# Splitting the first two loads of a streaming SiLU-multiply kernel between two DMA rings: by partition halves in place of rows

## The chip, the cores and the metric

The kernel runs on one core of a Trainium2 chip. The metric is the device time of one execution in microseconds (us); lower is better. The kernel before takes 471.45 us, the median of 3 runs that lie between 471.27 and 471.53 us. Another execution was profiled: it took 471.39 us, and its span, from the first to the last instruction in the trace, is 469.3 us.

## The reference

The input `x` has 32 x 512 rows of 2048 float32 values. Each row is cut in two halves of 1024; the output is SiLU of the first half times the second half.

```python
def reference(x):
    half_dim = x.shape[-1] // 2
    x1, x2 = x[..., :half_dim], x[..., half_dim:]
    silu_x1 = x1 * (1 / (1 + np.exp(-x1)))
    return (silu_x1 * x2).astype(np.float32)
```

The input is 134.22 MB and the output 67.11 MB. Each byte is moved once.

## The kernel before

The 16384 rows are cut into 16 tiles of 1024 rows. A tile puts K = 8 neighbouring rows into each of the 128 partitions, so a partition of an input tile `xt` holds 64 KB that also lie in one piece in memory, and a partition of an output tile `ot` holds 32 KB. There are two buffers for `xt` and two for `ot`. A full input tile is 8 MB (8,388,608 bytes), an output tile 4 MB.

Each tile is loaded, passed through SiLU on ScalarE (`silu`, line 78, from `xt` to `ot`), multiplied in place on VectorE (`mul`, line 85), and stored. The order of the instructions is written out by hand (`manual_schedule`). Two engines start transfers: SyncE (SP in the profile) and ScalarE (ACT). Each has a ring of its own, and the rings feed the same 16 DMA engines; SP's ring is q1 in the trace, ACT's is q10. The rule of the steady part is: SP starts the loads, ACT the stores. After tile i's last multiply, ACT starts the store of tile i and SP the load of tile i+2 into the buffer that has come free (lines 102 to 104).

The beginning is different, because there is no store yet with which loads could share the engines. There both rings carry loads (`load`, lines 67 to 75). Of tile 0, SP takes the first four rows of every partition (4 MB) and ACT the other four. Of tile 1, SP takes six rows of eight (6 MB) and ACT two. SP's part of tile 1 is cut once more into two transfers, one for the even and one for the odd partitions (`LOADED_IN`, line 31). That makes five transfers before the first computation: three on SP, two on ACT. Tile 0 is computed in four chunks of two rows (`KC_FIRST`, line 28), each with a SiLU and a multiply of 128x2048 values.

The end is different too: the last tile is computed in chunks of 2, 2 and 4 rows (`LAST`, line 29), and each chunk is stored by SP as soon as it is multiplied. Behind those stores `settle_all_but` (lines 57 to 65) puts an empty instruction on SP that waits until every transfer has landed except the last n; n is 3 here, the number of the last tile's stores. What then remains open is awaited by the end of the program (line 138).

Of the kernel before, what the change touches and what calls it, by code (L numbers as in the profile page):

```python
# [1 line left out]

# [4 lines left out]


@with_exitstack
def kernel(  # L10
    ctx: ExitStack,
    tc: tile.TileContext,
    x: bass.AP,
    out: bass.AP,
):


    nc = tc.nc
    P = nc.NUM_PARTITIONS

    x_flat = x.flatten_outer_dims()
    out_flat = out.flatten_outer_dims()
    num_rows, in_cols = x_flat.shape
    half = in_cols // 2
    dt = x_flat.dtype

    K = 8
    KC_FIRST = 2
    LAST = (2, 2, 4)
    SHARED = {0: K // 2, 1: 3 * K // 4}  # L30
    LOADED_IN = {1: [slice(0, None, 2), slice(1, None, 2)]}
    PLAN = [K] * (num_rows // (P * K))

    in_pool = ctx.enter_context(tc.tile_pool(name="in_pool", bufs=2))
    out_pool = ctx.enter_context(tc.tile_pool(name="out_pool", bufs=2))

    plan = []
    row = 0
    for k in PLAN:
        plan.append((row, k))  # L40
        row += P * k
    assert row == num_rows
    n_tiles = len(plan)

    def view(flat, i):
        row0, k = plan[i]
        return flat[row0:row0 + P * k].rearrange("(p k) d -> p k d", k=k)

    ctx.enter_context(tc.manual_schedule())

    loaded = {}
    sent = []

    def move(queue, out, in_):
        sent.append(queue.dma_start(out=out, in_=in_).ins)  # L55

    def settle_all_but(n):
        rest = nc.sync.nop(nofuse=True)
        for ins in sent[:-n]:
            tc.add_manual_dep(  # L60
                rest.ins,
                ins.name,
                mybir.DependencyInfo(mybir.DependencyClass.Sync, mybir.DependencyReason.DATA),
                reason="sync sees each earlier transfer land before the last ones",
            )

    def load(i):
        xt = in_pool.tile([P, K, in_cols], dt, name="xt")
        xv = view(x_flat, i)
        cut = SHARED.get(i, K)  # L70
        for ps in LOADED_IN.get(i, [slice(None)]):
            move(nc.sync, xt[ps, :cut], xv[ps, :cut])
        if cut < K:
            move(nc.scalar, xt[:, cut:], xv[:, cut:])
        loaded[i] = xt

    def silu(ot, xt, c, ce):
        nc.scalar.activation(  # L78
            out=ot[:, c:ce, :],
            in_=xt[:, c:ce, :half],  # L80
            func=mybir.ActivationFunctionType.Silu,
        )

    def mul(ot, xt, c, ce):
        nc.vector.tensor_mul(  # L85
            out=ot[:, c:ce, :],
            in0=ot[:, c:ce, :],
            in1=xt[:, c:ce, half:],
        )

    load(0)
    load(1)
    for i in range(n_tiles):
        xt = loaded.pop(i)
        ov = view(out_flat, i)
        ot = out_pool.tile([P, K, half], dt, name="ot")
        if i < n_tiles - 1:
            kc = KC_FIRST if i == 0 else K
            for c in range(0, K, kc):
                silu(ot, xt, c, c + kc)  # L100
                mul(ot, xt, c, c + kc)
            move(nc.scalar, ov, ot)
            if i + 2 < n_tiles:
                load(i + 2)
            continue
        c = 0
        for kc in LAST:
            silu(ot, xt, c, c + kc)
            mul(ot, xt, c, c + kc)
            move(nc.sync, ov[:, c:c + kc], ot[:, c:c + kc])  # L110
            c += kc
        settle_all_but(len(LAST))


# [1 line left out]
_INS = ['x']  # L116
_OUTS = [((32, 512, 1024), 'float32')]


# [23 lines left out]
```

## Time and profile before

| What | Value |
|---|---|
| median of 3 runs | 471.45 us (471.27 to 471.53) |
| the profiled execution | 471.39 us |
| its span | 469.3 us, so 2.1 us lie outside |
| VectorE busy | 139.5 us (30%), 21 multiplies |
| ScalarE busy | 114.2 us (24%), 21 activations and a table load |
| moved by DMA | 201.33 MB, mean 429 GB/s over the span |
| share of ring q1 (SP) and q10 (ACT) in the engines' time | 65.3% and 34.2% |

The profile's page cuts the span into 40 equal slices and gives for each the busy share of every engine and of the DMA engines. The list of waits tells which instruction stood idle and what ended the idle time. The chain that ended last follows the work back from the last instruction, at each step to what released it. The DMA list gives for every kind of transfer its size and the median time from the start of its issue to its landing; a transfer that is queued behind others on its ring counts that time as well. All times within the profile are counted from the start of the span.

### The profile page before, as it was taken

The numbers are of one execution on the slowest core, as the hardware profiler recorded it, in microseconds if no ns is written. First come the engines' busy times: TensorE is split into PE (matmuls) and PEld (weight loads), VectorE is DVE, ScalarE is ACT, GpSimd is POOL, SyncE is SP. The second block draws the span as 40 slices with busy tenths as digits, with TensorE's granted clock in tenths as the row PEclk, the third lists the DMA queues.
The fourth block names the chain that finished last, engine by engine and source line by source line (L and its number), as shares of the span: only waits on it lengthen the run. The fifth ranks groups of instructions, "written<-read, shape, count | busy, mean of one in ns | idle before, by whom it ended". The sixth has DMA issues, their size and how long they took to land.

```text
span 469.3 us, 190 instructions
## 1 busy us (share of the span) xinstructions
DVE 139.5 (30%) x21; ACT 114.2 (24%) x22; POOL 0.2 (0%) x4
## 2 busy tenths in 40 slices
DVE  0070702407024070330704307042070520605142
ACT  1053205032050410504105050050501405014060
POOL 0000000000000000000000000000000000000000
DMA  8999999999999999999999999999999999999988
GB/s 357 424 469 391 458 402 433 416 492 402 413 436 486 408 402 447 486 408 402 444 455 441 402 438 422 480 402 424 424 486 408 405 444 480 413 402 444 466 386 357
DMA packets 5200, 201.33 MB, mean 429 GB/s; under 512 B 592, under 2 KB 592, under 8 KB 592
## 3 DMA queue, kind: packets, MB, share of 16 engines
q1 hardware_dynamic: 2752, 132.12, 65.3%
q10 hardware_dynamic: 2448, 69.21, 34.2%
HBM read 134.22 MB, written 67.11 MB: 429 GB/s over the span
## 4 chain that ended last, share of the span: by engine, by line
DMA 72%; DVE 14%; ACT 12%; ACTq 0%; SPq 0%; issue 0%
DMA xt<-in_x_dram 72%; DVE ot L85 14%; ACT ot L78 12%; ACTq L138 0%; SPq L55 0%; ACTq L78 0%
## 5 line engine op out<-in xcount | busy, mean ns | idle before, releaser
L85 DVE TENSOR_TENSOR ot<-ot,xt 128x8192 f32<-128x8192 f32 (+2 forms) x21 | 139.5, 6659 | 321.4 <-ACT ot L78 321.4
L78 ACT ACTIVATE ot<-xt 128x8192 f32<-128x8192 f32 (+2 forms) x21 | 112.9, 5400 | 340.6 <-DMA xt<-in_x_dram 340.6
L78 ACT ACT_TABLE_LOAD x1 | 1.3, 1283 | 1.6 <-PEq L127 1.6
L127 POOL MEMSET const-bfloat16-1.0<- 128x1 bf16 x1 | 0.1, 101 | 0.0
L127 POOL MEMSET const-uint8-127<- 128x1 uint8 x1 | 0.1, 101 | 0.0
L127 POOL MEMSET const-float32-0.0<- 128x1 f32 x1 | 0.1, 98 | 0.2 <-issue 0.2
L127 POOL MEMSET const-float32-1.0<- 128x1 f32 x1 | 0.1, 98 | 0.0
## 6 DMA issues: line engine op xcount, KB each, us to landing
out_dram<-ot ACTq DMA_DIRECT2D x15, 4096.0 KB, 42.0
xt<-in_x_dram SPq DMA_DIRECT2D x2, 3072.0 KB, 36.4
xt<-in_x_dram ACTq DMA_DIRECT2D x1, 4096.0 KB, 22.1
xt<-in_x_dram SPq DMA_DIRECT2D x1, 4096.0 KB, 21.9
xt<-in_x_dram ACTq DMA_DIRECT2D x1, 2048.0 KB, 41.9
out_dram<-ot SPq DMA_DIRECT2D x2, 1024.0 KB, 7.8
out_dram<-ot SPq DMA_DIRECT2D x1, 2048.0 KB, 7.6
xt<-in_x_dram SPq DMA_DIRECT2D x14, 42.1
```

What stands on the lines that cost most here:

```text
L78: nc.scalar.activation(out=ot[:, c:ce, :], in_=xt[:, c:ce, :half], func=mybir.ActivationFunctionType.Silu,)
L85: nc.vector.tensor_mul(out=ot[:, c:ce, :], in0=ot[:, c:ce, :], in1=xt[:, c:ce, half:],)
L127: nc = _bacc.Bacc("TRN2", target_bir_lowering=False, num_devices=1)
```

## The change

Three things change.

First, the two rings share tiles 0 and 1 in another way. Every transfer now carries whole partitions of 64 KB, all eight rows. SP takes partitions 0 to 63 and ACT partitions 64 to 127, of both tiles; SP's part of tile 1 is cut into partitions 0 to 31 and 32 to 63. The number of transfers at the beginning stays five, three on SP and two on ACT, in the same order.

Second, after these loads are started, VectorE clears one column (`prime`, 128x1) and ScalarE applies SiLU to it, ahead of the first tile's work.

Third, SP's empty instruction at the end awaits all transfers but the last one, so the first two stores of the last tile are among those that it awaits.

```diff
-    SHARED = {0: K // 2, 1: 3 * K // 4}
-    LOADED_IN = {1: [slice(0, None, 2), slice(1, None, 2)]}
+    SHARED = {
+        0: ([slice(0, 64)], [slice(64, P)]),
+        1: ([slice(0, 32), slice(32, 64)], [slice(64, P)]),
+    }
...
         xv = view(x_flat, i)
-        cut = SHARED.get(i, K)
-        for ps in LOADED_IN.get(i, [slice(None)]):
-            move(nc.sync, xt[ps, :cut], xv[ps, :cut])
-        if cut < K:
-            move(nc.scalar, xt[:, cut:], xv[:, cut:])
+        on_sync, on_scalar = SHARED.get(i, ([slice(0, P)], []))
+        for ps in on_sync:
+            move(nc.sync, xt[ps], xv[ps])
+        for ps in on_scalar:
+            move(nc.scalar, xt[ps], xv[ps])
         loaded[i] = xt
...
     load(0)
     load(1)
+    prime = ctx.enter_context(tc.tile_pool(name="prime_pool", bufs=1)).tile([P, 1], dt, name="prime")
+    nc.vector.memset(prime, 0.0)
+    nc.scalar.activation(out=prime, in_=prime, func=mybir.ActivationFunctionType.Silu)
...
-        settle_all_but(len(LAST))
+        settle_all_but(1)
```

## The prediction

> **What bounds the kernel now.** I read the page's slices first, then the chain that ended last, the DMA list, and the stretches between two landings. The slices:
>
> ```profile
> span 469.3 us, 190 instructions
> ...
> DVE 139.5 (30%) x21; ACT 114.2 (24%) x22; POOL 0.2 (0%) x4
> ...
> DMA  8999999999999999999999999999999999999988
> ...
> DMA xt<-in_x_dram 72%; DVE ot L85 14%; ACT ot L78 12%; ACTq L138 0%; SPq L55 0%; ACTq L78 0%
> ```
>
> The DMA engines are busy from end to end, while the two computing engines are idle for 70% and more. The chain shows the same in its links: a tile's work of 15.7 us (SiLU 7.0, multiply 8.7) lets a buffer go, then a load runs for 42 us, and so on. The 42 us are not this transfer alone; the load shares the engines with the load ahead of it and with a store. So one tile costs what its 12.58 MB (8.39 in, 4.19 out) cost on 16 full engines, and the stretches between two landings show it:
>
> ```profile
> 43.20:72.20 29.00, 8.69 (x1) 7.03 (x1) 0.00 (x0) 1.00 1.00 434
> 72.20:101.20 29.00, 8.69 (x1) 7.03 (x1) 0.00 (x0) 1.00 1.00 434
> ...
> 391.20:420.20 29.00, 8.69 (x1) 7.03 (x1) 0.00 (x0) 1.00 1.00 434
> ```
>
> The columns are stretch, length, busy time of VectorE, ScalarE and GpSimd, clock, DMA share, GB/s. Each tile takes 29.00 us at 434 GB/s. All 201.33 MB at this pace are 464.0 us. The first packet starts at 1.74 us by the trace's packet records, so a perfect stream would end at 465.7; the last packet ends at 468.15. Only 2.4 us of the span are lost in the stream: the first packet of each engine takes 1.27 to 2.19 us where the same 32 KB take 1.21 later (0.59 too long on average), one packet on each engine between 39 and 42 us takes 0.87 us too long (2.6 to 2.9 instead of 1.815), and the rest goes into the engines' spread and the small packets of the last stores. Then 1.2 us of waits and barriers close the span, and 2.05 lie outside (471.39 - 469.34). The profiled run is 0.06 us below the median of 471.45; that is within the runs' spread.
>
> The beginning is what the change touches:
>
> ```profile
> xt<-in_x_dram SPq DMA_DIRECT2D x2, 3072.0 KB, 36.4
> xt<-in_x_dram ACTq DMA_DIRECT2D x1, 4096.0 KB, 22.1
> xt<-in_x_dram SPq DMA_DIRECT2D x1, 4096.0 KB, 21.9
> xt<-in_x_dram ACTq DMA_DIRECT2D x1, 2048.0 KB, 41.9
> ```
> ```profile
> 0.72 0.90 ACTq L55 DMA_DIRECT2D xt<-in_x_dram  x2
> 1.65 1.28 ACT L78 ACT_TABLE_LOAD   x1 [1.65 <-PEq L127]
> 22.65 7.31 ACT L78 ACTIVATE ot<-xt 128x2048 f32<-128x2048 f32 x4 [19.72 <-DMA xt<-in_x_dram]
> 24.59 8.90 DVE L85 TENSOR_TENSOR ot<-ot,xt 128x2048 f32<-128x2048 f32 x4 [24.59 <-ACT ot L78]
> 33.52 0.38 ACTq L55 DMA_DIRECT2D out_dram<-ot  x1
> 43.34 7.03 ACT L78 ACTIVATE ot<-xt 128x8192 f32<-128x8192 f32 x1 [13.38 <-DMA xt<-in_x_dram]
> ```
>
> Size and time to landing in the first fence, start and length in the second. Both halves of tile 0 land 22 us after issue, tile 1's last parts together at 43.2. By the packet records each engine takes one packet from each ring in turn, both rings run dry together at 42 us, and load 2 and store 0 have waited in them since 33.5: the engines never stop.
>
> **The change, part by part.**
>
> Shares of tiles 0 and 1. Bytes, number of transfers, their order and their rings' balance stay: 4 + 4 MB for each tile in place of 4 + 4 and 6 + 2, so that with turns of one 64 KB packet both rings still end together. What is new is that a transfer writes 64 or 32 neighbouring partitions. The trace has no such transfer. Its nearest rows are the two 3 MB transfers of tile 1, each on 64 partitions, every second one. They used all 16 engines (16 landings each), and their 48 KB packets took 1.815 us, 27.1 GB/s on each engine, the pace of the 128-partition packets (64 KB in 2.418 us). From that side the price is 0. The gain beyond it is the packet count: 256 packets in place of 512; 64 KB take 2.414 us from start to start, two of 32 KB 2 x 1.209, so 0.004 us on each of 16 per engine, -0.06 us. From the other side, the rows of a packet that is held up: the first packets reach 1.81 times their normal time (2.193 to 1.211). If two engines always got in each other's way at the same partitions, a packet would take twice as long. An engine has 16 packets of 64 KB in both tiles (16.78 MB / 16 / 64 KB), so the ends are 16 x 2.414 x 0.81 = +31 and 16 x 2.414 = +38.6 us, all on the path, since the stream is the bound. I take the near row, 0, as it differs only in which 64 partitions are written: of its 8 packets on each engine, the first seven took 1.815 us on all 16, and the eighth is the late one of 39 to 42 us.
>
> [...]
>
> Issue. The 64-partition issues on SP take 0.52 and 0.58 us in the trace, the 128-partition ones 0.37 to 0.46. If tile 0's issue takes longer before its first packet, that moves the stream by 0 to +0.2 us. I take 0: the first packet comes 1.02 us after the issue starts, long after the 0.37 us are over. The later issues have until 21 us.
>
> First SiLU. It used to wait for SP's half of tile 0 only and started at 22.65; now every chunk needs both halves, and the other half landed at 22.79. So tile 0's work ends some 0.15 us later, at 33.65, and with it store 0 (on ACT) and load 2 (on SP) are issued. Cover: the rings hold tile 1's packets until 42 us. Without that cover it would cost 0.15.
>
> The early activation. The clear (nearest row: a 128x1 clear on GpSimd, 0.1 us) runs on VectorE, idle until 24.59. The table load is already at 1.65, ahead of every load's landing, so nothing is brought forward. The activation of one column lasts at most the 1.9 us of the 128x2048 row; it ends before 6 us, and ACT next has work at 22.8. The cover is 17 us; without it the cost would be under 2 us.
>
> The end, in the waits of SP's queue (total, times, longest):
>
> ```profile
> SPq L138 <- DMA out_dram<-ot: 7.0, 2, 4.8
> ```
>
> SP issues the last store at 460.94, then waits. Now the empty instruction also waits for the two earlier stores (landed by 461.4 and 463.7). Behind it on SP there is only the end of the program, which waits for the last store at 468.5 anyway; nobody else waits for it. One wait instruction may drop out after the last landing; in the trace two such waits are 0.065 us apart. So 0 to -0.07; I take -0.03.
>
> Sum: 471.39 - 0.06 - 0.03 = 471.30, and with the parts' bounds (issue +0.2, end -0.04 more, the runs' spread) 471.1 to 471.7.
>
> **The rivals.**
>
> A, halves clash all along (slower). For it: no row shows neighbouring partitions, and all engines start with SP's ring within 0.8 us, so all write the lower half at the same time and then all the upper half. Against it: the even-partition row. It decides if two engines serving the same group of partitions run at less than 27.1 GB/s each. The pairs' head starts, some 0.3 us of each packet, take off 5 us: +31 to +38.6, about 471.3 + 35 = 506. If four engines met at once, a packet would take four times as long, 16 x 2.414 x 3 = +116, about 587.
>
> B, a clash that settles (slower). One of two engines falls behind by one packet, after which one writes the lower half while the other writes the upper half. Each such loss is one packet, 2.41 us; once or for a few packets in each tile, +2.4 to +15, about 474 to 486.
>
> C, the 0.87 us of 39 to 42 us do not recur (faster). They fell on the last packets of tile 1's odd partitions, which no longer exist. With the sum's -0.09 this gives 470.4, just past the bound for faster. Against it: a packet of the other ring that was under way was 0.16 us late as well, so it looks like a pause of the whole memory, not of this transfer.
>
> D, the change does nothing that shows: this is my forecast, since the engines were full and stay full.
>
> **How the numbers follow.** No change 0.38; A 0.27 (0.20 for two engines, 0.07 for four); B 0.20; C 0.10; an unseen 1 to 2 us at the beginning 0.05. From no change a measurement tells about 0.2%, 0.94 us. Faster is C with a little of the rest, 0.11; slower is A, B and the unseen, 0.51 with what of the forecast goes astray; same 0.38. The single likeliest case is no change, 471.3, with its own range of 471.1 to 471.7, though the slower cases together weigh more. The range of 8 in 10 goes from C's 470.4 to A's 508, leaving out the four-engine clash and part of the two ends.
>
> **What the profile after would show.** Right: both halves of tile 0 landing about 22 us after issue, tile 1's last part at 42 to 43, the first SiLU at 22.8, load 2 issued at 33.6, stretches of 29.00 us afterwards, the last store issued some 7.6 us before its landing. Wrong by A: 220 GB/s in the first slices, tile 0 at about 40 and tile 1 at 75 to 80, and then the same 29.00 us per tile, the whole loss in the first two tiles. Wrong by B: the same places, with a few us. Wrong by C: tile 1 at 42.3 and everything after it 0.9 earlier. If the stretches after 80 us differ from 29.00, my picture of the bound is wrong.

## The result and the profile after

The changed kernel takes 510.94 us (median of 5 runs, 509.54 to 511.25); the kernel before, 471.45 us in 5 runs beside it (471.27 to 471.66). The ratio is 1.083, 95% interval 1.0816 to 1.0847: 39.5 us slower. The span grew from 469.3 to 509.0 us.

The page of the changed kernel, with the slices of the DMA engines' busy share and of their GB/s:

```profile
span 509.0 us, 191 instructions
...
DMA  9797989999999999999999999999999999999998
GB/s 247 165 247 165 247 175 345 469 409 456 412 453 412 453 412 453 412 453 412 453 412 453 412 453 412 453 412 453 417 448 422 443 433 433 443 422 458 407 435 348
```

The engines are as busy as before, but in the first six slices, 12.7 us each, they move half as much: 165 to 247 GB/s. Busy share says that packets are under way, not how fast they go. The same in stretches (columns as in the prediction: stretch, length, busy time of VectorE, ScalarE, GpSimd, clock, DMA share, GB/s). A stretch counts a packet where it starts, so a share can pass 1 and the GB/s are a few per cent off, more in a stretch of a few us:

```profile
2.00:40.00 38.00, 0.00 (x0) 1.49 (x2) 0.00 (x0) 1.00 1.04 221
41.00:80.00 39.00, 8.90 (x4) 7.31 (x4) 0.00 (x0) 1.00 1.02 215
80.80:109.80 29.00, 8.69 (x1) 7.03 (x1) 0.00 (x0) 1.00 1.01 434
...
459.00:488.00 29.00, 8.69 (x1) 7.03 (x1) 0.00 (x0) 1.00 1.00 434
```

The kernel before moved this from 2 to 40 us:

```profile
2.00:40.00 38.00, 8.90 (x4) 8.24 (x5) 0.00 (x0) 1.00 1.02 431
```

From tile 2 on, nothing has changed: 29.00 us a tile at 434 GB/s. The whole loss lies in the loads of tiles 0 and 1. The timeline (start, length) dates it:

```profile
2.21 1.28 ACT L97 ACT_TABLE_LOAD   x1 [2.21 <-issue]
3.50 0.20 ACT L97 ACTIVATE prime<-prime 128x1 f32<-128x1 f32 x1
43.33 7.31 ACT L80 ACTIVATE ot<-xt 128x2048 f32<-128x2048 f32 x4 [39.62 <-DMA xt<-in_x_dram]
45.27 8.90 DVE L87 TENSOR_TENSOR ot<-ot,xt 128x2048 f32<-128x2048 f32 x4 [44.41 <-ACT ot L80]
54.20 0.36 ACTq L57 DMA_DIRECT2D out_dram<-ot  x1
82.90 7.03 ACT L80 ACTIVATE ot<-xt 128x8192 f32<-128x8192 f32 x1 [32.26 <-DMA xt<-in_x_dram]
```

Tile 0's first SiLU begins at 43.33 in place of 22.65, tile 1's at 82.90 in place of 43.34. Half of the loss falls on each tile, and nearly all of the 39.7 us by which the span grew are there by 82.9 us (39.6).

The packet records of the trace show how. A 64 KB packet of these loads takes 4.95 us in the median, and much the same on every engine, where one of a whole-tile load takes 2.418. An engine has 16 of them: 16 x 2.53 = 40.5 us. Add 0.3, since the first packet starts at 2.05 in place of 1.74. Take off what the kernel before lost here on its own account, 0.87 for the pause at 39 to 42 us and 0.59 for the first packets. That leaves 39.3 us, of the 39.7 measured. The two rings took turns packet by packet, with one place near 60 us where two of ACT's followed each other, and ended together, as before.

### The profile page after: what moved, and what is told of

Same layout as the page of the kernel before. It is cut to its first block, busy times and chain, and to the rows that moved or that the text cites. A ratio compares the mean times of both kernels' runs of the same rounds, so it can differ in the third digit from the quotient of the medians.

```text
span 509.0 us, 191 instructions
## 1 busy us (share of the span) xinstructions
DVE 139.6 (27%) x22; ACT 114.4 (22%) x23; POOL 0.2 (0%) x4
## 4 chain that ended last, share of the span: by engine, by line
DMA 66%; DVE 15%; ACT 11%; another core or an unknown queue 6%; ACTq 0%; issue 0%
DMA xt<-in_x_dram 66%; DVE ot L87 15%; ACT ot L80 11%; ACTq L143 0%; ACTq L57 0%; ACTq L80 0%
```

## The experiments

The theory after the result: what counts is which partitions a transfer writes. In the changed kernel they were all neighbours within one half of the 128, at 4.95 us for 64 KB; the even and odd partitions of the kernel before took 1.815 us for 48 KB, which is 2.42 for 64 KB. The rivals: some other part of the change; small or 64-partition transfers as such; the turns between the rings; the engines' all being in the same half at the same time. Two of the runs below have ten times each, and an interval; the others have one time each. The kernel before took 471.4 to 471.6 us beside them, and the differences read from single times are 9 us and more. The runs that change tile 0 keep the early activation and the new wait at the end.

**The halves alone.** The changed kernel without the early activation and with the old wait at the end.

```diff
-    nc.vector.memset(prime, 0.0)
-    nc.scalar.activation(out=prime, in_=prime, func=mybir.ActivationFunctionType.Silu)
...
-        settle_all_but(1)
+        settle_all_but(len(LAST))
```

> Tiles 0 and 1 are shared by partition halves as in the changed kernel; the early activation and the longer wait at the end are left out. Theory: the whole 39.5 us lies in the halves, so 510 to 511.5 us, tile 0 landing at 43 us, 64 KB packets of 4.95 us. Rival (part of the loss is in the early activation or the wait): under 508 us.

Measured: 509.77 us, a quarter of a us under the range and within the changed kernel's own spread (509.54 to 511.25), with packets near 4.88 us. The halves alone carry the loss.

**The rest alone.** The kernel before with the two other edits.

```diff
     load(1)
+    prime = ctx.enter_context(tc.tile_pool(name="prime_pool", bufs=1)).tile([P, 1], dt, name="prime")
+    nc.vector.memset(prime, 0.0)
+    nc.scalar.activation(out=prime, in_=prime, func=mybir.ActivationFunctionType.Silu)
...
-        settle_all_but(len(LAST))
+        settle_all_but(1)
```

> The kernel before with the early activation and the wait for all but the last store, its loads unchanged. Theory: nothing on the path, 471.2 to 471.6 us, ratio 0.999 to 1.001; the span's end after the last landing about 0.06 us shorter. Rival: over 473 us.

Measured: 471.48 us, ratio 0.9998 (0.9989 to 1.0007). No difference can be told, as expected.

**Even and odd.** The changed kernel, every transfer on other partitions, with numbers and sizes alike.

```diff
-        0: ([slice(0, 64)], [slice(64, P)]),
-        1: ([slice(0, 32), slice(32, 64)], [slice(64, P)]),
+        0: ([slice(0, P, 2)], [slice(1, P, 2)]),
+        1: ([slice(0, P, 4), slice(2, P, 4)], [slice(1, P, 2)]),
```

> The changed kernel with other partitions: SP takes the even ones and ACT the odd ones of both tiles, SP's part of tile 1 in two transfers of every fourth partition. Number and size of the transfers and packets are the same. [...] Rival (transfers on 64 or fewer partitions are slow when they meet one another, whichever partitions these are): 510 us.

Measured: 471.83 us, ratio 1.0005 (0.9995 to 1.0015), not the rival's 510: the whole loss is gone, though two transfers of 64 partitions each still meet on the two rings, and SP loads its part of tile 1 by 32 partitions at a time. From 2 to 40 us:

```profile
2.00:40.00 38.00, 8.90 (x4) 8.79 (x6) 0.00 (x0) 1.00 1.07 442
```

This is the clearest run of the study. Same ring, same bytes, same packets; only which partitions are written differs, and the pace doubles, from 221 to 442 GB/s.

**The middle.** Tile 0: SP loads partitions 32 to 95, ACT the two outer quarters; tile 1 by rows as in the kernel before (the lines for tile 1 are left out of this and the next diffs of that kind, which show the new line alone).

```diff
-    SHARED = {
-        0: ([slice(0, 64)], [slice(64, P)]),
-        1: ([slice(0, 32), slice(32, 64)], [slice(64, P)]),
-    }
+    SHARED = {0: ([slice(32, 96)], [slice(0, 32), slice(96, P)])}
```

> Tile 0: SP takes partitions 32 to 95 (neighbours too, but half of them below 64 and half above), ACT takes 0 to 31 and 96 to 127 in two transfers; tile 1 as in the kernel before. [...] Rival (64 neighbouring partitions are slow wherever they lie): both near 4.95, +20 us, 491.5. Rival (the turns between lower and upper half cost): 471.5, since no turn is between the two halves.

Measured: 482.63 us, far from both rivals. If the outer quarters alone are slow, an engine has four packets of 4.95 us in place of 2.418, +10.1 us on the 471.57 of the kernel before: 481.7, an estimate from these packet times, and 0.9 under the measured time. In the packet records the outer quarters' packets take 4.4 to 5.4 us; the middle's take 2.418 where all engines are on them (14.7 to 17.5 us) and 2.5 to 3.6 where some engines are still in an outer quarter. In stretches, with such a time of the middle first, then a mixed one, then tile 1:

```profile
14.50:17.00 2.50, 0.00 (x0) 0.00 (x0) 0.00 (x0) 1.00 0.98 419
17.50:32.00 14.50, 0.00 (x0) 0.00 (x0) 0.00 (x0) 1.00 0.78 231
33.00:43.00 10.00, 7.04 (x4) 7.31 (x4) 0.00 (x0) 1.00 1.00 431
```

So 64 neighbours are not slow as such: these, half of them below partition 64 and half above, took 2.418 us a packet.

**One ring.** Tile 0's two halves go one after the other on SP; tile 1 as before.

```diff
+    SHARED = {0: ([slice(0, 64), slice(64, P)], [])}
```

> Tile 0: SP loads both halves one after the other, ACT nothing of it; tile 1 as in the kernel before, by rows on both rings. So at no time do two rings carry different halves. [...] Rival (the loss needs two rings that take turns between halves): 471.5 us.

Measured: 496.66 us. The turns between the rings are not needed for the loss. It is 5 us more than 491.8, an estimate from eight packets on each engine at 4.95 us in place of 2.418 and the 471.58 of the kernel before. The packets of the upper half took 5.12 us where nothing else was under way (from 33 us on), and the 16 KB packets of tile 1 on ACT's ring, which write all 128 partitions, took 1.0 to 1.3 us between 10 and 24 us in place of 0.61: a slow transfer also slows its neighbour.

**Blocks of 16, and every eighth.** Two ways to cut tile 0 into eight transfers of 16 partitions, tile 1 as before.

```diff
+    SHARED = {0: ([slice(0, 16), slice(16, 32), slice(32, 48), slice(48, 64)],
+                  [slice(64, 80), slice(80, 96), slice(96, 112), slice(112, 128)])}
```

> Tile 0 in eight transfers of 16 neighbouring partitions, four on SP (0 to 63), four on ACT (64 to 127); tile 1 as in the kernel before. [...] Rival (only the halves count): packets of 4.95, +20 us, 491.5 us.

```diff
+    SHARED = {0: ([slice(0, P, 8), slice(1, P, 8), slice(2, P, 8), slice(3, P, 8)],
+                  [slice(4, P, 8), slice(5, P, 8), slice(6, P, 8), slice(7, P, 8)])}
```

> Tile 0 in eight transfers of 16 partitions each, every eighth one (0, 8, 16 ... on SP, up to 4, 12, 20 ... on ACT); tile 1 as in the kernel before. [...] Rival (only neighbours, or only the halves, are slow): packets of 2.42, 471.6 us.

Measured: 524.72 us for the blocks, 490.26 for every eighth. Their stretches in which tile 0 was loaded, the blocks first:

```profile
2.00:73.00 71.00, 0.00 (x0) 1.49 (x2) 0.00 (x0) 1.00 0.97 111
```
```profile
2.00:40.00 38.00, 0.00 (x0) 1.49 (x2) 0.00 (x0) 1.00 1.04 221
```

A block of 16 neighbours runs at a quarter (packets of 9.24 us in place of 2.418, 53 us lost). Every eighth partition runs at one half (packets of 4.90), although it covers both halves of the partitions and has no neighbours. So neither neighbourhood nor the halves are the point, and the number of partitions is not either: these are two sets of 16 partitions with a pace of 111 and 221 GB/s, by the packet times 113 and 214 (16 x 64 KB in 9.24 and 4.90 us). What tells a slow set from a fast one is not shown by these runs; they show the pace of each set that was tried.

One thing these loads can't separate. Partition p's data lie 64 KB x p into the tile in DRAM, so the partitions that are written and the addresses that are read change together. The length of the piece read is not it, since the middle and the lower half are one piece of 4 MB each; that certain addresses are slow to read remains possible, and only the next run bears on it.

**Stores by halves.** The kernel before, with the stores of four tiles cut in two.

```diff
+            if i in (5, 6, 7, 8):
+                move(nc.scalar, ov[:64], ot[:64])
+                move(nc.scalar, ov[64:], ot[64:])
+            else:
+                move(nc.scalar, ov, ot)
```

> The kernel before, with the stores of tiles 5 to 8 cut into a lower and an upper half, both on ACT; no load is changed. [...] Rival (only writing into the memory is slowed): 471.5 us.

Measured: 480.95 us, 9.4 us for four stores, where the rival had none. The cut stores' packets run from 187 to 316 us; the first stretch still has the full pace, the next four have not:

```profile
187.00:216.00 29.00, 8.69 (x1) 7.03 (x1) 0.00 (x0) 1.00 1.03 434
216.00:245.00 29.00, 8.69 (x1) 7.03 (x1) 0.00 (x0) 1.00 0.98 414
245.00:274.00 29.00, 8.69 (x1) 7.03 (x1) 0.00 (x0) 1.00 1.00 412
274.00:303.00 29.00, 8.69 (x1) 7.03 (x1) 0.00 (x0) 1.00 1.01 408
303.00:332.00 29.00, 5.38 (x1) 7.03 (x1) 0.00 (x0) 1.00 1.00 400
```

Reading the on-chip memory by halves costs too, but only some 2.3 us a store here. The cut stores' 32 KB packets took 1.22 to 1.42 us in the mean of a store, in place of 1.21, and so were far from doubled; whole-tile loads took turns with them on the other ring, and some of those loads' 64 KB packets took up to 4.4 us in place of 2.42. In the output, partition p lies 32 KB x p into the tile, so these halves are other pieces of DRAM than the loads' halves. That they are slowed as well speaks for the partitions as the cause and not the addresses; it is one run, and no store was cut in another way beside it.

**Late engines.** Why do all packets take twice as long, when an engine that comes early could be alone in its half until a second one, its partner, comes there? Two runs shifted some engines against the others by one small load ahead on SP's ring. Its data isn't used. In both, SP's half of tile 1 is one transfer; that line is left out of the diffs.

```diff
+    early = out_pool.tile([P, K, half], dt, name="ot")
+    move(nc.sync, early[0:P:16].rearrange("p k d -> p (k d)"), x_flat[0:32].rearrange("(p k) d -> p (k d)", k=4))
     load(0)
```

> The changed kernel with one more load ahead of the others on SP's ring, 32 KB into each of 8 partitions, which occupies 8 of the 16 DMA engines for 1.2 to 2.5 us (its data is overwritten and not used), and with SP's half of tile 1 in one transfer. Theory (the loss is a matter of all engines being at the same half at the same time): with 8 engines late by about a packet, some write the lower half while others write the upper one, and most of the 39 us are won back, 473 to 485 us. [...]

```diff
+    early = ctx.enter_context(tc.tile_pool(name="early_pool", bufs=1)).tile([P, 128], dt, name="early")
+    move(nc.sync, early[0:127], x_flat[0:127, 0:128])
     load(0)
```

> The changed kernel with SP's half of tile 1 in one transfer, and one small load ahead on SP's ring: 512 bytes into each of 127 partitions, whose data is not used. [...] Theory 2 (an engine's pace in such a transfer doesn't depend on when its partner comes): all 16 stay at 4.9 to 5.0; 511 to 514 us.

Measured: 516.20 us with eight late engines, 514.43 with one. In the first, the records show two groups of eight engines about 2 us apart from 14 us on, so that for some 60% of the time one group wrote the lower half and the other the upper. All 16 still took 4.9 to 5.1 us a packet. In the second, from 9 to 42 us, one engine ran 2 to 3 us apart from the other 15 and took the upper half while they took the lower; it, and all others, stayed at 4.94 to 5.15. In both, the stretches show no gain:

```profile
14.00:73.00 59.00, 8.90 (x4) 7.31 (x4) 0.00 (x0) 1.00 1.00 211
```
```profile
12.00:42.00 30.00, 0.00 (x0) 0.00 (x0) 0.00 (x0) 1.00 1.02 214
```

So the picture of engines that meet at the same half at the same time falls. A shift doesn't bring the pace back. The times lie 5.3 and 3.5 us above the changed kernel's 510.94, the second 0.4 above theory 2's range; the first packets beside the small loads took up to 7.2 and 6.1 us.

**Eight engines in small transfers.** On SP, tile 0 starts with four transfers of 8 partitions each, every fourth one of 0 to 31, and partitions 32 to 63 follow in one. ACT takes 64 to 127 in one transfer; tile 1 is as before.

```diff
+    SHARED = {0: ([slice(0, 32, 4), slice(1, 32, 4), slice(2, 32, 4), slice(3, 32, 4), slice(32, 64)],
+                  [slice(64, P)])}
```

> [...] Theory 2 (a packet into one half is slow in itself, as no shift of the engines changed it): 4.9 us. The time of the whole lies between 485 and 500 us by either, since the engines are no longer evenly loaded.

Measured: 499.26 us, and theory 2's 4.9 us fits a part of the packets alone. Of the small transfers' packets the first eight took 5.1 us (from 6.4 us on), while the other eight engines were loading partitions 64 to 127. The second eight took 6.4 to 6.8 us (from 21.5 us on), while the others loaded partitions 32 to 63, and the third eight 2.7 to 3.3 us, when the others had begun tile 1. The last eight took 2.42 us (from 37.9 us on), while the other engines loaded tile 1 by even partitions. The stretches around the two:

```profile
2.00:34.00 32.00, 0.00 (x0) 1.42 (x2) 0.00 (x0) 1.00 1.03 208
38.00:40.00 2.00, 0.00 (x0) 0.00 (x0) 0.00 (x0) 1.00 1.14 492
```

And when the first eight engines later loaded partitions 32 to 63 (from 41.5 us on), the others' 48 KB packets of even or odd partitions rose from 1.82 to 3.6 us. The time of a packet thus depends on what the other engines are doing: in these small transfers, 5.1 us beside partitions 64 to 127 and 2.42 beside even partitions. No run here shows why. Which engine serves which partition of a half transfer can't be read from these traces, so the mechanism behind the doubling stays open. What is shown is how fast each set of partitions was loaded when all engines were at work on such sets.

## Why the prediction was wrong

The forecast was no change, 471.3 us, in a range up to 508; the time is 510.9.

- **What bounds the kernel.** Right: the stretches after tile 1 still take 29.00 us, and what the first loads lost went into the time undiminished.
- **The shares of tiles 0 and 1.** This is the step that failed: "I take the near row, 0, as it differs only in which 64 partitions are written". That difference is the whole effect. The row of every second partition was near in shape, count and size, and far in the one property that the change altered. The text itself said that no row shows neighbouring partitions, and still took this row's value. The runs put in its place: 2.05 times the packet time for 0 to 63, 0 to 31 and 64 to 127, against 1.00 for even and odd and for 32 to 95.
- **Both halves at once.** The two loads took 80.8 us from the first packet to tile 1's landing, against 41.5 in the kernel before (1.74 to 43.2). A packet took 5.12 us for one half alone, on one ring, and 4.95 for both at once, 3% less: the second ring brought next to nothing.
- **Rival A.** Its signs and its place came as described: half the rate in the first slices (221 GB/s from 2 to 40 us), tile 0 at about 40 (43.3), tile 1 at 75 to 80 (82.8), then 29.00 us a tile. Its size, 35, was the middle of its two ends, and what kept it from the upper one was "The pairs' head starts, some 0.3 us of each packet, take off 5 us". Nothing comes off: the engines were 0.65 us apart and all took the same 4.95 us, and the runs with late engines show that even a shift by 2 us brings nothing. Its upper end gives 471.3 + 38.6 = 509.9, and the range stopped short of it, at 508. The condition it named, engines that meet, is not what was found: out of step by 2 to 3 us, they still took 4.9 to 5.15 us a packet.
- **Rival B**, a clash that settles, fell: the last packets of tile 1 are as slow as the first, 4.94 and 4.95 us in the median.
- **Rival C**, no pause at 39 to 42 us: with even and odd partitions, where those packets no longer exist, the last packets of tile 1 still lost 1.15 us at 39 us. What pauses there is open.
- **Issue.** The first packet came 0.3 us later, past the bound of 0.2: a 64-partition issue took 0.54 us in place of 0.37. The run with even and odd partitions starts at 2.06 us as well, and no difference of its time can be told.
- **First SiLU, early activation, end.** The column's activation takes 0.20 us at 3.50, and the clear 0.06 at 0.80, both under the cover named. At the end the empty instruction waits 2.3 us for the second store, and the program then for the last one. The waits of SP's queue (total, times, longest):

```profile
SPq L143 <- DMA out_dram<-ot: 4.7, 1, 4.7
SPq L60 <- DMA out_dram<-ot: 2.3, 1, 2.3
```

They are the 7.0 us of the kernel before in another order: 0.79 us from the end of the last wait to the span's end, against 0.80. So the 0.03 us were 0.01, and the run with these two edits alone shows no difference.

## What to carry to other kernels

A load's pace here depended on which partitions it touches, not on how many, as long as the other engines were at work on sets of the same kind: 16 neighbours ran at a quarter (111 GB/s), 64 neighbours in one half and every eighth partition at a half (221), and even or odd partitions, or 64 across the middle, at full pace (442 and 419). Beside a slow transfer, a fast one slowed down too (16 KB packets 1.0 to 1.3 us in place of 0.61). When a load like this one must be shared between two rings, cut it by rows (471.45 us here) or by even and odd partitions (471.83); the two complementary halves at the same time (510.94) didn't add up. And before a near row of the trace is used as a price, ask whether it differs from the new operation in the one thing that is being changed.

## What the runs showed of the hardware that was not expected

- Busy DMA engines (a share of 1.04 from 2 to 40 us) moved 221 in place of 431 GB/s with no gap between packets; only the GB/s row and the packet times tell.
- Two groups of engines in different halves for 60% of the time, or one engine apart from the rest, left every packet at 4.9 to 5.15 us.
- Transfers into all partitions, or into even or odd ones, are slowed by a slow one beside them: 16 KB packets 1.0 to 1.3 us in place of 0.61, 48 KB packets 3.6 in place of 1.82.
- Stores cut by halves cost 2.3 us each beside whole-tile loads.
